# Both down-projections of a two-layer decoder wholly in pairs of chunks by seven products

## The chip, the cores and the metric

The kernel runs on one core of a Trainium2 chip. The core has TensorE (PE, the matrix engine, with its weight load shown apart as PEld), VectorE (DVE), ScalarE (ACT), GpSimd (POOL) and SyncE (SP, which only issues transfers). All of them read and write the on-chip memory; matmuls add up in eight banks of PSUM. The metric is the device time of one execution in microseconds (us).

## The reference

It is a decoder trunk of two layers over 512 tokens of width 1024. Layer 0 has a dilated attention of three head groups, layer 1 a forgetting attention (FoX) whose keys and values are projected once from the stream behind layer 0. Behind each attention stands a gated FFN with a convolution over three tokens. In short:

```python
def conv_ffn(xn, w_up, cw, cb, w_down):
    a = xn @ w_up                                   # 512 x 5632
    ap = jnp.pad(a, ((0, 0), (CONV_W - 1, 0), (0, 0)))
    a = sum(ap[:, j:j + T] * cw[j] for j in range(CONV_W)) + cb
    gate, val = jnp.split(a, 2, axis=-1)
    return (jax.nn.gelu(gate, approximate=True) * val) @ w_down   # 512 x 2816 by 2816 x 1024

for l in range(DEPTH):
    g = norm_gains[l]
    if l < N_A:
        mix = dilated_mixer(rms_norm(h, g[0]), w_qkv_a[l], w_o_a[l], cos, sin)
    else:
        if l == N_A:
            kvf = rms_norm(h, kv_norm) @ w_kvf      # keys, values, forget gates
            ...
        mix = fox_mixer(rms_norm(h, g[0]), w_q_b[j], w_o_b[j], k_sh, v_sh, c_sh)
    h = h + rms_norm(mix, g[1])
    f = conv_ffn(rms_norm(h, g[2]), w_up[l], conv_w[l], conv_b[l], w_down[l])
    h = h + rms_norm(f, g[3])
```

All is fp32. The change concerns the last product of `conv_ffn`, the down-projection, once per layer.

## The kernel before

**Products.** Every operand of a product is kept as a pair: a high part, rounded to the type that PE multiplies fast, and a low part, the rest. `mm3` (L258) makes a product of three matmuls: high by high (L259), high by low (L260), low by high (L261). A weight of 128 x 1024 is loaded raw by SP, copied to its high part by ACT (L53), and DVE subtracts that for the low part (L59). The class `Weights` (W) holds the list of all weights in the order of use and loads some of them ahead; `split` makes both parts, `take` hands out raw ones.

**Memory.** Tiles rotate through pools of fixed slots: `t8` (8 KB per partition, 17 slots), `t4` (4 KB, 9) and `t2` (2 KB, 6). Whoever asks for the next tile of a pool waits until the oldest user of that slot has finished. Each engine works off its own instructions in the order in which the program writes them.

**The down-projection.** The 2816 rows of `w_down` are 22 chunks of 128 (NF), the tokens 4 blocks of 128, the columns 2 halves of 512, so that the output fills all eight banks. ND = 8 pairs of chunks go by seven products in place of eight: a pair of chunks by two pairs of token blocks and two halves of columns is a product of 2 x 2 blocks, and sums of blocks are multiplied in the place of some blocks. The sums of the weights are made early (`down_sums`, L528: three loads, four subtractions on DVE L543 to L546, two stores) and kept in DRAM (`dT`). The sums of the activations are made in `pair_sums` (L705) from the activations that the FFN's first half stored in DRAM (`hD`, stored by POOL L610). There are two phases. In the first, `mul_one` (L752) makes four of the products of all pairs, 24 matmuls a pair. Then `combine_one` (L761) adds the banks to one another, and in the second `mul_two` (L771) adds the other three products, 18 matmuls a pair; its operands are prepared by `pair_two` (L730), from activations that stay in `t8` all the time (`dkeep`) and a fourth weight sum that `load_t4` (L725) brings back.

The 6 other chunks are plain, 24 matmuls each (`Proj`, L345): two of them between the phases, the last R = 4 at the end. For these four, `Proj.finish` (L375) runs over the blocks of tokens 0, 1, 2, 3 and their halves, 12 matmuls each, and hands each finished half to the boundary that follows. Two of the plain weights are made with an adding transfer by POOL (`high_added`, L70) in place of DVE.

**The boundary.** Behind layer 0, `SharedBoundary` (L433) takes the halves: `Mix` (L284) squares and scales them (ACT L299, DVE L306), adds the block to the stream (L313); then the block is normed (L441) and transposed (L446, low parts L463) for the values and keys. The values (`v_ps`, from L1290) start with blocks 0 and 1 while blocks 2 and 3 are still being transposed. Behind layer 1, `Final` (L474) stores the blocks; its last half is done in two parts of 256 columns.

**Where the sums of weights are made.** 16 pairs in two runs: `down0` (L1181) in the attention of layer 0, ten pairs, in `t8` tiles and stored through SP's queue, a step after each group of matmuls (L1172); `down1` (L1388) while the keys and values are made, six pairs, in `t4` tiles and stored through POOL's queue.

The few lines that set the end of the down-projection before:

```python
for b in range(NB):
    for hf in range(2):
        ...
        for i in range(self.R):
            ...
            self.step(n + i, b, hf)
        bd.half(b, hf, self.banks[b, hf])
```

Of the kernel before, what the change touches and what calls it, by code (L numbers as in the profile page):

```python
# [16 lines left out]
NB = 4  # L17
# [10 lines left out]
ND = 8  # L28
# [63 lines left out]
def trunk_kernel(ctx, tc, x, norm_gains, w_qkv_a, w_o_a, w_q_b, w_o_b, kv_norm, w_kvf, b_f,  # L92
# [62 lines left out]
    def add_ffn(l):  # L155
        for c in range(NF):
            add_cols(w_up[l], c * 128)
            add_cols(w_up[l], DFF + c * 128)

        for j in range(ND):  # L160
            add(lambda raw, j=j: [(raw[:, 0:512], w_down[l][j * 256:j * 256 + 128, 0:512]),
                                  (raw[:, 512:1024], dT[l][j, :, 0:512])])
            add(lambda raw, j=j: [(raw, dT[l][j, :, 512:1536])])
        plain = [*range(2 * ND, NF)]
        add_rows(w_down[l], [*plain[:2], *range(1, 2 * ND, 2), *plain[2:]])
# [118 lines left out]
    class Mix:  # L284
# [5 lines left out]
        def half(self, b, hf, o):  # L290
            if hf == 0:
                self.st[b] = (small(2, "ss"), t4([128, D], name="mix"), small(1, "sd"), small(1, "vr"))
            self.part(b, hf, o, H2[hf], hf == 1)
# [51 lines left out]
    class Proj:  # L345
# [3 lines left out]
        def __init__(self, KC, R, get_act, begin=0, banks=None):  # L349

            self.KC, self.R, self.get_act, self.begin = KC, R, get_act, begin
            self.w, self.banks, self.done = {}, {} if banks is None else banks, set()

        def weight(self, kc):
            while self.begin + len(self.w) <= kc:
                self.w[self.begin + len(self.w)] = W.get()
            return self.w[kc]

        def step(self, kc, b, hf, part=slice(0, 512)):
# [3 lines left out]
            c = slice(hf * 512 + part.start, hf * 512 + part.stop)  # L363
            if kc == 0:
                self.banks[b, hf] = bank([128, 512], name="acc")
            mm3(self.banks[b, hf][:, part], ah[:, s], al[:, s], w[0][:, c], w[1][:, c],
                kc == 0, kc == self.KC - 1, part.start > 0 or self.begin > 0)
# [7 lines left out]
        def finish(self, bd, ahead, hook=None):  # L375
            n = self.KC - self.R
            if hook is None:
                for kc in range(self.begin, n):
# [10 lines left out]
            for b in range(NB):  # L389
                for hf in range(2):  # L390
                    if bd.narrow == (b, hf):
                        for q, part in enumerate((slice(0, 256), slice(256, 512))):
                            for i in range(self.R):
                                self.step(n + i, b, hf, part)
                            bd.part(b, 1 + q, self.banks[b, hf][:, part], part)
                        continue
# [4 lines left out]
                    bd.half(b, hf, self.banks[b, hf])  # L401
            W.ahead = 4

    class Boundary:


        narrow = None
# [6 lines left out]
        def half(self, b, hf, o):  # L414
            self.mix.half(b, hf, o)
            if hf == 0:
                if b >= 2:
                    self.transpose(b - 2)
                if b >= 1:
                    self.norm(b - 1)  # L420
            else:
                self.mix.add(b)
# [10 lines left out]
    class SharedBoundary(Boundary):  # L433

        def __init__(self, gain_mix, gains, name):
            super().__init__(gain_mix, None, name)
            self.gains = gains

# [5 lines left out]
        def transpose(self, b):  # L446
# [13 lines left out]
            for i, xf in enumerate(xfs):  # L460
                hi, lo = self.xT[0][i][:, :, s], self.xT[1][i][:, :, s]
                act.copy(hi, xf)
                dve.tensor_tensor(lo, xf, hi.bitcast(F32), ALU.subtract)  # L463
            for i, pt in enumerate(pts):
# [9 lines left out]
    class Final:  # L474


        narrow = (NB - 1, 1)
# [7 lines left out]
        def half(self, b, hf, o):  # L485
            self.mix.half(b, hf, o)
            if hf:
                self.out(b)
# [39 lines left out]
    def down_sums(pairs, place, queue, behind):  # L528
# [3 lines left out]
        for i in range(n + 1 + behind):  # L532
# [8 lines left out]
            if 1 <= i <= n:  # L541
                a, b = live[i - 1]
# [4 lines left out]
            i -= 1 + behind  # L547
# [20 lines left out]
    def ffn(l, bd, cp, nxt, ahead):  # L568
        hD = tc.dram_tile([NF, 128, T], F32, name="hD")
        hraw, hs, hc = {}, {}, {}  # L570

        def load_h(j):
            if j < NF // 2:
                hraw[j] = t4([128, 2, T], name="hraw")
                sp.dma_start(hraw[j], hD[2 * j:2 * j + 2].rearrange("c p t -> p c t"))

        def prep(j):
            if j < NF // 2:
                load_h(j + 1)
                hs[j] = t = t8([128, 2, 2, T], F32R, name="hs")  # L580
                src = hraw.pop(j)
                act.copy(t[:, 0], src)
                dve.tensor_tensor(t[:, 1], src, t[:, 0].bitcast(F32), ALU.subtract)

        def get_act(kc):
            if kc % 2 == 0 and kc // 2 + 1 not in hs:
                prep(kc // 2 + 1)
            return hs[kc // 2][:, 0, kc % 2], hs[kc // 2][:, 1, kc % 2]
# [104 lines left out]
        keep, one, two = {}, {}, {}  # L693
        H = slice(0, 512), slice(512, 1024)

        a11, s1_, s3_, s2_, a12, a22 = (slice(i * 256, i * 256 + 256) for i in range(6))
        sums, t4r = {}, {}

        def pair_load(j):
            if j < ND:  # L700
                keep[j] = k = t8([128, 1536], name="dkeep")
                sp.dma_start(k[:, 0:512], hD[2 * j])
                sp.dma_start(k[:, 1024:1536], hD[2 * j + 1])

        def pair_sums(j):  # L705

            pair_load(j + 1)
            k = keep[j]
            dve.tensor_tensor(k[:, s3_], k[:, a11], k[:, s1_], ALU.subtract)
            dve.tensor_tensor(k[:, s1_], k[:, s1_], k[:, a22], ALU.add)  # L710
            dve.tensor_tensor(k[:, s2_], k[:, s1_], k[:, a11], ALU.subtract)

        def pair_highs(j):

            src = [*W.take(2), keep[j][:, 0:1024]]
            one[j] = [t8([128, 2, 1024], F32R, name="w") for _ in range(3)]
            for w, r in zip(one[j], src):
                act.copy(w[:, 0], r)
            sums[j] = src

        def pair_lows(j):
            for w, r in zip(one[j], sums.pop(j)):
# [7 lines left out]
        def pair_two(j):  # L730

            r1, = W.take(1)
            load_t4(j + 1)
            k, r4 = keep.pop(j), t4r.pop(j)
            w, ac = (t8([128, 2, 1024], F32R, name="w") for _ in range(2))
            t4p = t4([128, 2, 512], F32R, name="wsum")
            act.copy(w[:, 0], r1)
            dve.tensor_tensor(k[:, s2_], k[:, a12], k[:, s2_], ALU.subtract)
            act.copy(t4p[:, 0], r4)
            act.copy(ac[:, 0, 0:768], k[:, 768:1536])  # L740
            dve.tensor_tensor(w[:, 1], r1, w[:, 0].bitcast(F32), ALU.subtract)
            dve.tensor_tensor(t4p[:, 1], r4, t4p[:, 0].bitcast(F32), ALU.subtract)
            dve.tensor_tensor(ac[:, 1, 0:768], k[:, 768:1536], ac[:, 0, 0:768].bitcast(F32), ALU.subtract)
            two[j] = ac, w, t4p
# [3 lines left out]
        def product_of(o, ac, q, w, c, bp, first):  # L748
            s = slice(q * 256 + bp * 128, q * 256 + bp * 128 + 128)
            mm3(o, ac[:, 0, s], ac[:, 1, s], w[:, 0, c], w[:, 1, c], first, False, True)  # L750

        def mul_one(j, bp):  # L752
            wa, wb, ac = one[j]
# [17 lines left out]
        def mul_two(j, bp):  # L771
            ac, w, t4p = two[j]
            product_of(db[bp, 0], ac, 1, w, H[0], bp, False)
            product_of(db[bp + 2, 0], ac, 2, t4p, H[0], bp, False)
            product_of(db[bp, 1], ac, 0, w, H[1], bp, False)
# [5 lines left out]
        def down_pairs(po):  # L781
            n = 2 * ND
# [4 lines left out]
            for j in range(1, ND - 2):  # L787
# [3 lines left out]
                if j + 3 < ND:  # L791
# [3 lines left out]
                    if j + 3 == ND - 1:  # L795
                        load_h(ND)
                elif j + 3 == ND:
                    pair_lows(j + 2)
                if j == ND - 3:
                    W.high_added()  # L800
            W.high_added()
            prep(ND)
            load_t4(0)
            for bp in range(2):
                for j in (ND - 2, ND - 1):
                    mul_one(j, bp)
                combine_one(bp)
            one.clear()
            W.n_get += n
            pair_two(0)  # L810
            for bp in range(2):
                for kc in (n, n + 1):
                    for b in (bp, bp + 2):
                        po.both(kc, b)
            pair_two(1)
            for j in range(ND):
                if j < ND - 2:
                    pair_two(j + 2)
                if j == ND - 1:
                    W.n_get += ND  # L820
                if j >= ND - 2:
                    W.split(W.n_split + 2)
                for bp in range(2):
                    mul_two(j, bp)
                del two[j]
# [85 lines left out]
        po = Proj(NF, 4, get_act, 2 * ND, db)  # L911
        down_pairs(po)
        W.ahead = 4
        po.finish(nxt, ahead)
# [167 lines left out]
    def v_proj0(between):  # L1082
        banks = []
        ws = [[t.rearrange("p (k c) -> p k c", k=4) for t in W.get()] for _ in range(2)]
        for b in range(4):
# [9 lines left out]
            if b % 2:  # L1095
                act.copy(V[0][:, b - 1:b + 1, :], banks[b // 2])
                for f in between[b // 2]:
                    f()

# [47 lines left out]
    transpose0(3)  # L1147
    qk0(2, 2, 3)
    W.split(5)
    qk_post(0, 2, qk_banks[2])  # L1150
    qk0(3, 0, 1, 2, 3)
# [5 lines left out]
    def wide_proj(g, name, post, between):  # L1157

        banks = [bank([128, T], name=name) for _ in range(4)]
        for s in range(4):  # L1160
# [11 lines left out]
            next(down0, None)  # L1172
# [8 lines left out]
    down0 = down_sums([(0, j) for j in range(ND)] + [(1, j) for j in range(10 - ND)], in_one, sp, 1)  # L1181
    v_proj0([[L(qk_transpose, 0, 0), L(qk_transpose, 0, 1)],
# [97 lines left out]
    def keep_values(hf, b, o):  # L1280
        if b == 0:
# [3 lines left out]
    bd2.norm(3)  # L1285
    banks = [bank([128, 512], name="v_ps") for _ in range(4)]
    wv = []
    W.ahead = 1
    for sp_, blocks in ((0, (0, 1)), (2, (0, 1)), (0, (2,)), (2, (2,)), (0, (3,)), (2, (3,))):
# [325 lines left out]
```

## Time and profile before

| what | value |
|---|---|
| median of 3 runs | 1135.58 us (1135.26 to 1135.85) |
| the profiled execution's own time | 1135.51 us |
| its span | 1133.4 us |
| PE busy | 1120.9 us, 99% |
| DVE busy | 859.9 us, 76% |
| ACT busy | 601.4 us, 53% |
| POOL busy | 176.9 us, 16% |
| down-projection of layer 0 in the trace | 418.1 to 529.3 us |
| down-projection of layer 1 in the trace | 1017 to 1127.7 us |

The span goes from the first to the last instruction; the execution's own time is 2.1 us longer. "L259" is line 259 of the kernel above. A row of the timeline gives the start, the length, the engine, the line, the operation and the tiles (written <- read), and in brackets the idle time of the engine before it with what ended it. A row of a group gives the number of instructions, then the busy time in us and the mean of one in ns, then the idle time before them. A row of transfers gives how many there are, the size of each, and the median time from issue to landing. "dkeep", "w", "acc" and so on are the program's names of tiles.

### The profile page before, as it was taken

Reading aid. Unit: us, or ns where it says so; the run is one execution under the profiler, and the core shown is the slowest. Engines: PE = TensorE matmul, PEld = TensorE weight load, DVE = VectorE, ACT = ScalarE, POOL = GpSimd, SP = SyncE. Lnnn points to the kernel's source line nnn. Section 1 sums busy time; section 2 is a strip of 40 time slices with the busy share of each in tenths; the row PEclk is TensorE's granted clock in tenths of the full one; section 3 lists DMA queues with packets and bytes.
Section 4 is the critical chain, followed back from the end, with each engine's and each line's share of the span. In section 5 each row is a group of like instructions: output and inputs, shape, how many; then the busy total and the mean of one; then the engine's idle time right before and its main releaser. Section 6 shows DMA issues by size and latency. Waiting matters only on the chain.

```text
span 1133.4 us, 16992 instructions
## 1 busy us (share of the span) xinstructions
PE 1120.9 (99%) x6306; PEld 956.8 (84%) x6306; DVE 859.9 (76%) x1385; ACT 601.4 (53%) x1018; POOL 176.9 (16%) x259
## 2 busy tenths in 40 slices
PE   9999999999999999999999999999999999999997
PEld 6888889889899888888778888789889899888886
DVE  6558788887888588866587788848888888679754
ACT  5454565454544555655552677756444344455642
POOL 1833002200000100000001566500300000110000
PEclk9999999999999999999999999999999999999999
DMA  9269664334434778763348644363433443788732
GB/s 301 88 225 392 244 171 130 94 103 123 147 103 131 226 220 315 204 195 92 116 149 286 198 121 122 95 208 105 119 102 93 139 141 99 201 260 302 196 122 75
DMA packets 164780, 191.36 MB, mean 169 GB/s; under 512 B 9305, under 2 KB 123465, under 8 KB 164698
## 3 DMA queue, kind: packets, MB, share of 16 engines
q1 hardware_dynamic: 156442, 161.96, 45.0%
q0 software_dynamic: 8256, 28.32, 8.7%
q8 instruction: 50, 0.82, 0.3%
q14 instruction: 32, 0.26, 0.1%
HBM read 149.30 MB, written 30.46 MB: 159 GB/s over the span
## 4 chain that ended last, share of the span: by engine, by line
PE 83%; DVE 6%; issue 6%; ACT 3%; DMA 1%; POOL 1%; DVEq 0%; POOLq 0%; ACTq 0%
PE up L259 13%; PE up L260 12%; PE up L261 12%; PE acc L259 8%; PE acc L261 8%; PE acc L260 8%; PE qk_ps L260 2%; PE qk_ps L259 2%; PE qk_ps L261 2%; DVE w L59 1%; PE first L261 1%; PE first L259 1%; PE first L260 1%; PE v_ps L259 1%; PE v_ps L261 1%
## 5 line engine op out<-in xcount | busy, mean ns | idle before, releaser
L59 DVE TENSOR_TENSOR w<-wraw,w 128x1024 fp32r<-128x1024 f32 x110 | 141.1, 1301 | 34.6 <-ACT w L53 34.0
L594 ACT ACTIVATE bb<-up,conv 128x512 f32<-128x512 f32 x80 | 60.7, 776 | 153.2 <-PE up L261 77.0
L53 ACT CAST w<-wraw 128x1024 fp32r<-128x1024 f32 x110 | 112.5, 1048 | 23.8 <-DMA wraw<-in_w_up_dram 7.1
L259 PE MATMUL up<-xch,w 128*128 128x512 f32 (+1 forms) x292 | 104.9, 359 | 0.0
L260 PE MATMUL up<-xbl,w 128*128 128x512 f32 (+1 forms) x292 | 104.8, 359 | 0.0
L259 PE MATMUL up<-xbh,w 128*128 128x512 f32 (+1 forms) x292 | 104.8, 359 | 0.0
L260 PE MATMUL up<-xcl,w 128*128 128x512 f32 (+1 forms) x292 | 104.8, 359 | 0.0
L261 PE MATMUL up<-xbh,w 128*128 128x512 f32 (+1 forms) x292 | 104.7, 358 | 0.0
L261 PE MATMUL up<-xch,w 128*128 128x512 f32 (+1 forms) x292 | 104.7, 358 | 0.0
L610 POOL DMA_DIRECT2D hD<-hc x42 | 24.3, 594 | 343.4 <-DVE hc L612 343.4
L595 DVE SCALAR_TENSOR_TENSOR bb<-up,conv,bb 128x511 f32<-128x511 f32 x80 | 59.5, 743 | 20.9 <-ACT bb L594 20.9
L259 PE MATMUL acc<-w 128*128 128x512 f32 x192 | 74.7, 389 | 0.0
L260 PE MATMUL acc<-w 128*128 128x512 f32 x192 | 74.7, 389 | 0.0
L261 PE MATMUL acc<-w 128*128 128x512 f32 x192 | 74.7, 389 | 0.0
L259 PE MATMUL up<-xsh,w 128*128 128x256 f32 x224 | 63.4, 283 | 0.0
L260 PE MATMUL up<-xsl,w 128*128 128x256 f32 x224 | 63.4, 283 | 0.0
L261 PE MATMUL up<-xsh,w 128*128 128x256 f32 x224 | 63.4, 283 | 0.0
L259 PEld LDWEIGHTS up<-xch,w 128*128 128x128 f32 x292 | 55.1, 189 | 8.3
L261 PEld LDWEIGHTS up<-xbh,w 128*128 128x128 f32 x292 | 55.1, 189 | 8.3
L597 DVE SCALAR_TENSOR_TENSOR bb<-up,conv,bb 128x510 f32<-128x510 f32 x80 | 59.9, 749 | 2.8
L260 PEld LDWEIGHTS up<-xbl,w 128*128 128x128 f32 x292 | 55.1, 189 | 8.1
L259 PEld LDWEIGHTS up<-xbh,w 128*128 128x128 f32 x292 | 55.1, 189 | 8.2
(315 smaller groups left out, 3092.8 us busy)
## 6 DMA issues: line engine op xcount, KB each, us to landing
wraw<-in_w_up_dram SPq DMA_DIRECT2D x88, 512.0 KB, 4.6
wraw<-in_w_down_dram SPq DMA_DIRECT2D x28, 512.0 KB, 3.7
hD<-hc POOLq DMA_DIRECT2D x44, 256.0 KB, 4.7
dT<-dsums SPq DMA_DIRECT2D x20, 512.0 KB, 6.6
dsums<-in_w_down_dram SPq DMA_DIRECT2D x16, 512.0 KB, 7.7
dsums<-in_w_down_dram SPq DMA_DIRECT2D x32, 256.0 KB, 7.8
dkeep<-hD SPq DMA_DIRECT2D x32, 256.0 KB, 5.8
wraw<-dT SPq DMA_DIRECT2D x16, 512.0 KB, 5.9
```

The lines of the kernel that those rows point to most:

```text
L53: self.nc.scalar.copy(pair[:, 0], raw)
L59: self.nc.vector.tensor_tensor(pair[:, 1], raw, pair[:, 0].bitcast(F32), ALU.subtract)
L259: pe.matmul(o, ah, bh, start=first, stop=False, skip_group_check=shared)
L260: pe.matmul(o, ah, bl, start=False, stop=False, skip_group_check=shared)
L261: pe.matmul(o, al, bh, start=False, stop=last, skip_group_check=shared)
L594: act.activation(bb[:, s, :], ps, AF.Identity, bias=cp[:, 3, ch:ch + 1], scale=cp[:, 2, ch:ch + 1])
L595: dve.scalar_tensor_tensor(bb[:, s, 1:], ps[:, :T - 1], cp[:, 1, ch:ch + 1], bb[:, s, 1:], ALU.mult, ALU.add)
L597: dve.scalar_tensor_tensor(bb[:, s, 2:], ps[:, :T - 2], cp[:, 0, ch:ch + 1], bb[:, s, 2:], ALU.mult, ALU.add)
L610: pool.dma_start(hD[c - 1], hc.pop(c - 1))
```

## The change

All eleven pairs of chunks go by seven products (ND = 11), the plain chunks and their code are gone. Four things come with it.

First, the activations are no longer kept between the phases. The sum S2 of a pair is stored to DRAM (`sD`, through POOL's queue), and the second phase loads it again, with one chunk of activations and the fourth weight sum (`load_two`), one pair ahead. The pools have 16, 10 and 8 slots in place of 17, 9 and 6.

Second, the second phase is split into its three products, `p_21`, `p_11` and `p_12` (`p_1` is the last two). The blocks of tokens end in the order 2, 3, 0, 1. For the blocks 2 and 3, one half is already complete when the first phase's banks are added, the other ends with `p_21` of the last two pairs; `p_1` of the pairs 6 and 7 fills in behind each. For the blocks 0 and 1 the last three pairs (LAST) are held back, 9 matmuls for each half.

Third, the boundary and the values behind layer 0 follow that order, and the first four weights of the next stage are split inside the loop over the blocks, one for each.

Fourth, 22 weight sums are made. Two pairs are loaded right behind the first transposes of layer 0's attention, in `t4` tiles (`sums`); `down0` has ten pairs, with two steps between load and subtraction; `down1` seven pairs, from the values on; `down2`, new, has the last three pairs of layer 1 at the end of FoX attention.

```diff
-ND = 8
+ND = NF // 2
+LAST = 3
...
-    p8 = ctx.enter_context(tc.tile_pool(name="p8", bufs=17))
-    p4 = ctx.enter_context(tc.tile_pool(name="p4", bufs=9))
-    p2 = ctx.enter_context(tc.tile_pool(name="p2", bufs=6))
+    p8 = ctx.enter_context(tc.tile_pool(name="p8", bufs=16))
+    p4 = ctx.enter_context(tc.tile_pool(name="p4", bufs=10))
+    p2 = ctx.enter_context(tc.tile_pool(name="p2", bufs=8))
...
         def pair_sums(j):
...
             dve.tensor_tensor(k[:, s2_], k[:, s1_], k[:, a11], ALU.subtract)
+            pool.dma_start(sD[j], k[:, s2_])
...
-        def load_t4(j):
+        def load_two(j):
             if j < ND:
-                t4r[j] = t2([128, 512], name="dt4")
-                sp.dma_start(t4r[j], dT[l][j, :, 1536:2048])
+                later2[j] = k, r4 = t4([128, 768], name="dact2"), t2([128, 512], name="dt4")
+                sp.dma_start(k[:, 0:256], sD[j])
+                sp.dma_start(k[:, 256:768], hD[2 * j + 1])
+                sp.dma_start(r4, dT[l][j, :, 1536:2048])
...
+            last = range(ND - LAST, ND)
+            for j in range(2, ND - 2):
+                for bp in range(2):
+                    p_21(j, bp)
+                if 2 <= j - 2 < ND - LAST - 2:
+                    p_1(j - 2, 0)
+                    p_1(j - 2, 1)
+                    two.pop(j - 2)
+                pair_two(j + 3)
+            W.n_get += 3 * ND
+            for i, b in enumerate(nxt.order):
+                if ahead and i < 3:
+                    W.split(W.n_split + 1)
+                if b >= 2:
+                    nxt.half(i, 0, 1, db[b, 1])
+                    for j in range(ND - 2, ND):
+                        p_21(j, b - 2)
+                    nxt.half(i, 1, 0, db[b, 0])
+                    for bp in range(2):
+                        p_1(last[0] - 2 + i, bp)
+                    continue
+                for j in last:
+                    p_11(j, b)
+                nxt.half(i, 0, 0, db[b, 0])
+                if ahead and i == 3:
+                    W.split(W.n_split + 1)
+                parts = (slice(0, 256), slice(256, 512)) if nxt.narrow and i == NB - 1 else (slice(0, 512),)
+                for q, part in enumerate(parts):
+                    for j in last:
+                        p_12(j, b, part)
...
     class SharedBoundary(Boundary):
...
+        order = (2, 3, 0, 1)
...
+            if (i, n) == (3, 0):
+                self.transpose(self.order[1], lambda: self.norm(self.order[2]))
+            elif n == 0 and i >= 1:
+                self.norm(self.order[i - 1])
...
+            if (i, n) == (2, 1):
+                self.transpose(self.order[0])
...
-    def down_sums(pairs, place, queue, behind):
+    def down_sums(pairs, place, queue, lag, behind):
...
+    sums = down_sums([(0, 0), (0, 1)], in_two, sp, 1, 0)
...
-    down0 = down_sums([(0, j) for j in range(ND)] + [(1, j) for j in range(10 - ND)], in_one, sp, 1)
+    down0 = down_sums([(0, j) for j in range(2, ND)] + [(1, 0)], in_one, sp, 2, 1)
...
+    down1 = down_sums([(1, j) for j in range(1, 8)], in_two, pool, 1, 0)
...
-    down1 = down_sums([(1, j) for j in range(10 - ND, ND)], in_two, pool, 0)
...
+    down2 = down_sums([(1, j) for j in range(8, ND)], in_two, pool, 1, 0)
...
+        if n in (N - 1, N, N + 1, N + 2):
+            next(down2)
```

More of the change, by code (lines that the diff above doesn't have):

```diff
@@ L463, in transpose @@
                 dve.tensor_tensor(lo, xf, hi.bitcast(F32), ALU.subtract)
+            if later is not None:
+                later()
             for i, pt in enumerate(pts):
@@ L1150, in trunk_kernel @@
     qk_post(0, 2, qk_banks[2])
+    next(sums)
     qk0(3, 0, 1, 2, 3)
@@ L1171, in wide_proj @@
                 f()
-            next(down0, None)
+            if (g, name, s) != (1, "qk_ps", 1):
+                next(down0, None)
     def v_post(g, b, o):
```

234 lines of the change are left out of this document (108 added, 126 removed).

## The prediction

> **What bounds the kernel now.** I read the page's totals first, then the chain that ended last, then what TensorE waits for, then windows over the stages that the change touches, and single rows last.
>
> ```profile
> span 1133.4 us, 16992 instructions
> PE 1120.9 (99%) x6306; PEld 956.8 (84%) x6306; DVE 859.9 (76%) x1385; ACT 601.4 (53%) x1018; POOL 176.9 (16%) x259
> PE 83%; DVE 6%; issue 6%; ACT 3%; DMA 1%; POOL 1%; DVEq 0%; POOLq 0%; ACTq 0%
> ```
>
> TensorE (PE) is busy 99% of the span and is 83% of the chain. Its waits, by what it waited for (total us, times, longest), are these, longest first:
>
> ```profile
> PE o_ps L1503 <- ACT pT L1490: 1.5, 1, 1.5
> PE warm L220 <- DVE zero L215: 1.4, 1, 1.4
> PE acc L259 <- DVE mix L306: 1.1, 1, 1.1
> PE qk_ps L260 <- DVE w L59: 1.0, 2, 0.8
> ```
>
> None of them is in a down-projection except the third, at the kernel's end. So the time is the count of matmuls times their pitch: a matmul taken out is worth its pitch, unless something that was hidden comes late. The question is only what comes late. The windows give the length of the stretch, then busy time and count of PE, weight loads, DVE, ACT and POOL, then clock, share of the DMA engines, GB/s. The first two are the down-projection of layer 0: its first products, and all after them up to the next stage.
>
> ```profile
> 418.10:461.60 43.50, 43.50 (x193) 36.04 (x192) 33.87 (x44) 25.50 (x28) 2.30 (x3) 1.00 0.81 265
> 461.60:529.30 67.70, 67.28 (x305) 55.65 (x304) 52.01 (x72) 41.29 (x64) 0.00 (x0) 1.00 0.51 153
> ...
> 70.00:130.00 60.00, 59.84 (x336) 49.82 (x335) 45.84 (x114) 27.81 (x82) 18.09 (x32) 1.00 0.95 352
> 100.00:105.00 5.00, 5.00 (x28) 3.94 (x28) 3.46 (x4) 2.76 (x5) 3.69 (x7) 1.00 1.03 415
> ```
>
> The first says 192 matmuls in 43.5 us, 0.2266 us each, at clock 1.00. DVE, the third pair of numbers, is busy 33.87 of them (78%) and 52.01 of 67.7 (77%): it is the engine to watch. The last two are the attention of layer 0, where the DMA engines are nearly full.
>
> **The saving.** A pair of chunks costs 4 x 2 x 3 = 24 matmuls of first products and 3 x 2 x 3 = 18 of second ones, 42 in all, where two plain chunks cost 48. Three pairs per layer change over: 18 matmuls fewer per layer. In layer 1 the last half block runs in two parts of 256 columns; it shrinks from 4 chunks to 3 pairs' product, 2 x 3 matmuls of 256 columns fewer (as 3 wide ones), so 15 wide and 6 narrow.
>
> ```profile
> 1123.61 0.28 PE L261 MATMUL acc<-w,hs 128*128 128x256 f32 x1
> ...
> 1124.69 0.28 PE L261 MATMUL acc<-w,hs 128*128 128x256 f32 x1
> ```
>
> These stand nine matmuls apart: 1.08 / 9 = 0.12 us. Layer 0: 18 x 0.2266 = 4.08; layer 1: 15 x 0.2266 + 6 x 0.12 = 4.12. Together -8.2 us.
>
> The Trainium skill, page TensorE: Matmul & The Clock Gate, section Back-to-back issue gap, gives a sustained 131 ns for a matmul of 512 columns between weight loads. By it the 36 would save an estimated 4.7 us; the trace disagrees, at 227 ns.
>
> **First products, then second ones: are weights and activations ready?** DVE per pair:
>
> ```profile
> 425.82 0.42 DVE L709 TENSOR_TENSOR dkeep<-dkeep 128x256 f32<-128x256 f32 x1
> ...
> 439.79 0.42 DVE L709 TENSOR_TENSOR dkeep<-dkeep 128x256 f32<-128x256 f32 x1
> ...
> 462.71 0.70 DVE L769 TENSOR_TENSOR acc<-acc,dsum 128x512 f32<-128x512 f32 x1
> 467.40 0.42 DVE L738 TENSOR_TENSOR dkeep<-dkeep 128x256 f32<-128x256 f32 x1
> ...
> 479.18 0.41 DVE L738 TENSOR_TENSOR dkeep<-dkeep 128x256 f32<-128x256 f32 x1
> ```
>
> L709 opens a pair of the first phase; three pairs lie between the rows: 13.97 / 3 = 4.66 us, against 24 x 0.2266 = 5.44 us of PE. Three more pairs at 4.66 stay under PE's pace: nothing. L738 opens a pair of the second phase; four pairs: 11.78 / 4 = 2.95 us of DVE against 18 x 0.2266 = 4.08 of PE. The first phase ends at 418.1 + 264 x 0.2266 = 477.9. The last sum (L769) ended at 463.41, 1.8 us behind its phase; so after the change at about 479.9. From there eight pairs of the second phase remain for DVE (3 to 10): 479.9 + 8 x 2.95 = 503.5. PE asks for pair 10 after 36 (pairs 0, 1) + 42 (p_21 of 2 to 8) + 48 (p_1 of 2 to 5) + 3 (p_21 of pair 9) = 129 matmuls: 477.9 + 29.2 = 507.1. Slack 3.6 us; a pitch of 3.4 us a pair uses it up. On this side the plain chunks' cover is gone (they gave PE work while the second products' operands were made), and it is replaced by eight pairs' p_21 and p_1 running behind each other.
>
> What can make the pitch longer is the loading: per pair now the weight row (512 KB), a chunk of activations (256), the sum S2 from DRAM (128) and the weight sum (256), 1.18 MB. At the 415 GB/s of the window 100 to 105 that is 2.84 us, at the 352 of 70 to 130 3.35, at the 265 of the first phase 4.45, though there the engines were busy only 0.81 (327 at full share, 3.61). I take 3.35, the nearest row with full engines: just inside. For the first pairs, whose loads start while phase one still loads, +0.3 us; bounds 0 and the rival below.
>
> The Trainium skill, page DMA: Bandwidth & Descriptors, section Bandwidth, puts transfers of 1 MB at 341 GB/s and advises to batch to 1 MiB or more, while these are 128 to 512 KB. By its figure a pair takes an estimated 3.46 us, some 0.4 us a layer late; the window of 415 GB/s, in transfers no larger, says that the size alone does not hold it there.
>
> **Stores by POOL.** 22 stores of S2 at some 0.58 us each are 12.8 us on an engine that is busy 16%; in layer 0's first phase it had 2.30 us of work in 43.5. Hidden, 0. The reload of S2 on SP waits for its store; behind it on SP stand that pair's two other loads and the next weights, but the store of pair 0 is nearly a whole first phase old by then, and of pair 10 several pairs' time.
>
> ```profile
> L610 POOL DMA_DIRECT2D hD<-hc x42 | 24.3, 594 | 343.4 <-DVE hc L612 343.4
> ```
>
> **The end of down 0.** Here lies the one cost that I expect on the path. Four weights of the next stage are split inside the loop over blocks, where before that was done ahead of it:
>
> ```profile
> 500.45 2.50 DVE L59 TENSOR_TENSOR w<-wraw,w 128x1024 fp32r<-128x1024 f32 x2 [1.98 <-ACT w L53]
> ...
> 510.77 0.60 ACT L299 ACTIVATE junk<-acc 128x512 bf16<-128x512 f32 x1 [2.03 <-PE acc L261]
> ...
> 539.51 1.29 DVE L463 TENSOR_TENSOR xkl<-xf,xkh 128x512 fp32r<-128x512 f32 x2
> ...
> 541.11 0.39 PE L259 MATMUL v_ps<-w,xkh 128*128 128x512 f32 x1
> ```
>
> and the same stretch as a window:
>
> ```profile
> 505.00:541.00 36.00, 35.58 (x170) 29.46 (x169) 23.27 (x43) 19.73 (x45) 0.00 (x0) 1.00 0.34 86
> ```
>
> From the read of the first block's second half (510.77) to the first low part of the third transposed block (539.51 + 0.65) the chain of mix, norm and transposes takes 29.4 us; PE has matmuls to cover it until 541.1, 30.3 us. After the change each of the last two blocks' halves is 9 instead of 12 matmuls, the cover shorter by some 6 x 0.2266 = 1.4: 28.9. Alone, the unchanged chain of 29.4 makes PE wait 0.5. Now the splits: 4 x 1.25 = 5.0 us of DVE (and 4 x 1.05 of ACT). In the window 505 to 541 DVE is idle 12.7 us, so all could hide (0.5 in all), or none (5.5), since that idle time sits inside the chain's own steps. The first two go ahead of blocks whose matmuls still leave a block's time, the others directly into the steps of the third and fourth: I take two of four, 0.5 + 2.5 = +3.0 us. The changed order of blocks (2, 3, 0, 1) only renames which transposes are last. In layer 1 nothing is split there, and the tail behind the last matmul stays: 0.
>
> **Weight sums at other places.** A pair's sums are four DVE instructions of 692 to 716 ns (first and last row):
>
> ```profile
> L543 DVE TENSOR_TENSOR dsums<-dsums 128x512 f32<-128x512 f32 x16 | 11.5, 716 | 0.0
> ...
> L546 DVE TENSOR_TENSOR dsums<-dsums 128x512 f32<-128x512 f32 x16 | 11.4, 711 | 0.9 <-DMA dsums<-in_w_down_dram 0.4
> ```
>
> Where the added ones go (a window, then single rows), and what a store of sums takes to land:
>
> ```profile
> 27.00:48.00 21.00, 21.00 (x146) 19.59 (x145) 9.75 (x9) 7.58 (x10) 20.84 (x22) 1.00 0.01 2
> ...
> 559.73 1.39 DVE L1265 TENSOR_TENSOR kst<-k_ps,kst 64x512 fp32r<-64x512 f32 x2 [6.67 <-ACT kst L1262]
> ...
> 746.03 0.69 DVE L1517 TENSOR_TENSOR OTb<-o_ps,OTb 128x512 fp32r<-128x512 f32 x1 [7.56 <-ACT OTb L1513]
> ...
> 762.36 0.60 ACT L299 ACTIVATE junk<-acc 128x512 bf16<-128x512 f32 x1 [1.71 <-PE acc L261]
> ...
> dT<-dsums SPq DMA_DIRECT2D x20, 512.0 KB, 6.6
> ```
>
> Six more pairs at some 2.8 us. Two are loaded in 27 to 48, where the DMA engines are 0.01 busy and DVE 46%; of ten in layer 0's attention (as many as before) only the place changes, in 16 slots instead of 17. One falls behind the values stage, whose keys leave DVE idle 6.67 us at a time. Three fall at the end of FoX attention: 8.5 us against one idle gap of 7.56, with w_o's weights queued on SP behind slots that a store holds 6.6 us (on POOL's queue, where these stores stand, nothing else is due until the next FFN's sums); ahead of 762.36 ACT idles 1.71 us for PE there, so a weight may come that much later. I take +0.3 for attention (-0.5 to +3, a store's half landing) and +0.4 for FoX (0 to +3).
>
> **Sum.** The profiled run took 1135.51 us (span 1133.4 and 2.1 around it), 0.07 below the median. 1135.5 - 8.2 + 0.3 (second products) + 3.0 (end of down 0) + 0.3 + 0.4 = 1131.3. About 0.2%, 2.3 us, is what a measurement of this kernel can tell from no change.
>
> **Rivals.** *The second products' loads bind.* Place: behind the last combine, both layers. At 4.45 us a pair (265 GB/s) pair 10 is ready at 479.9 + 35.6 = 515.5, 8.4 us late: two layers +16.8, 1148. It ends on the slower side from 3.41 + (4.2 + 2.3) / 16 = 3.8 us a pair, 310 GB/s. For it: the first phase moved 265; against it: 352 held for 60 us, and SP loads as far ahead as ten slots allow.
>
> *A slot late in attention 0 or at the end of FoX.* A weight's copy waits for a slot that a store of sums holds: one landing of 6.6 us less some 2 us of lead, 4.6: 1135.9, no change. In both places: 1140, slower. For it: 0.95 of the DMA engines' time taken there, one slot fewer; against it: PE waits there now only 1.0 us on a weight.
>
> *The boundary is fully exposed.* None of the splits hides, and the other two terms stand at their half: 1131.3 + 2.5 + 1.5 = 1135.3, no change.
>
> *A matmul taken out is worth less than its pitch*, since what runs beside it sets the pace: if each of the 33 wide and 6 narrow ones is worth only the 0.12 us of the narrow rows, they save 4.7, not 8.2: 1134.8, no change. The row of 192 matmuls in 43.5 us speaks against it. The figure that the Trainium skill's page TensorE: Matmul & The Clock Gate gives in the section Back-to-back issue gap comes to the same.
>
> **Chances.** Forecast 0.66. Loads bind 0.12 (slower). A slot late once 0.10 (same), twice 0.04 (slower). Boundary exposed 0.05 (same). Pitch 0.03 (same). Faster 0.66, same 0.18, slower 0.16. The forecast's own range: 1131.3 - 2.5 (splits hidden) - 1.5 (the others at their low ends) = 1127.3, up to 1134.5. The range to 1136.2 takes in the cases of no change and leaves the slower ones, 0.16, out.
>
> **What would show it.** Right: 528 matmuls of first products for the two layers at 0.227, the second phase without PE gaps, a gap of some 3 us at the third block of the values stage waiting for xkl, PE's sum of busy time 8 us less. Wrong: PE waiting in the second phase on the low parts (DVE) or on loads; gaps on w in the attention of layer 0 or at w_o; the splits found wholly in DVE's idle time (then 1128.3).

## The result, and the profile after

The changed kernel takes 1139.56 us (1139.24 to 1142.58), the one before 1135.58: a ratio of 1.0041, interval 1.0026 to 1.0056. It is slower by 4 us, where 1131.3 was forecast.

The totals of the page of the changed kernel, then its longest waits of TensorE:

```profile
span 1137.3 us, 17235 instructions
PE 1118.0 (98%) x6267; PEld 951.0 (84%) x6267; DVE 909.4 (80%) x1455; ACT 611.2 (54%) x1032; POOL 191.8 (17%) x285
```

```profile
PE o_ps L1535 <- ACT pT L1522: 2.6, 5, 1.5
PE v_ps L260 <- DVE w L60: 2.3, 2, 2.0
...
PE s_ps L1013 <- DVE qkT L989: 1.1, 1, 1.1
...
PE xt_ps L327 <- DVE xn L278: 1.0, 1, 1.0
PE pT_ps L1520 <- DVE nm L1496: 0.8, 2, 0.4
PE acc L260 <- DVE w L60: 0.8, 1, 0.8
PE v_ps L259 <- ACT xkh L470: 0.7, 1, 0.7
```

PE has 39 matmuls fewer, and waits that were not there before: for a weight's low part in the values of layer 0's attention (`v_ps` L260), for `qkT`, `xn`, `w` in w_o (`acc` L260), more often for `pT`. A stage is taken from its first matmul to the next stage's first one (attention 0: from the span's start; FoX: first scores to last output; w_o 1: from there to the FFN's first matmul; the tail: to the span's end). All stages of the two profiled executions, in us:

| stage | before | after | difference |
|---|---|---|---|
| attention 0 | 145.56 | 150.85 | +5.3 |
| w_o 0 and FFN 0 up | 272.52 | 272.54 | 0.0 |
| down 0 | 111.24 | 106.52 | -4.7 |
| values behind layer 0 | 23.56 | 25.87 | +2.3 |
| keys and second values | 81.12 | 81.10 | 0.0 |
| FoX loop | 111.09 | 113.10 | +2.0 |
| w_o 1 | 35.12 | 38.09 | +3.0 |
| FFN 1 up | 237.08 | 237.06 | 0.0 |
| down 1 and tail | 116.14 | 112.19 | -4.0 |

The down-projections gave what they should, 8.7 us. The four other differences add up to 12.6. The two phases of down 0 in the changed kernel, as windows, show that the new second phase has no hole: PE is busy through both, at clock 1.00.

```profile
423.40:483.22 59.82, 59.82 (x265) 49.54 (x264) 54.90 (x73) 36.83 (x41) 5.39 (x10) 1.00 0.83 292
483.22:529.90 46.68, 46.68 (x215) 38.82 (x214) 41.22 (x61) 32.88 (x54) 0.00 (x0) 1.00 0.69 228
```

The loss in the values behind layer 0 shows as two waits, for a low part of a weight and for a transposed block, and the rest, 1.3 us, as matmuls that stand further apart:

```profile
537.86 0.50 PE L260 MATMUL v_ps<-w,xkh 128*128 128x512 f32 x1 [0.29 <-DVE w L60]
543.59 0.50 PE L259 MATMUL v_ps<-w,xkh 128*128 128x512 f32 x1 [0.67 <-ACT xkh L470]
```

The largest loss is at the start of attention 0. DVE, POOL, SP and ACT of the changed kernel there:

```profile
31.42 1.61 DVE L554 TENSOR_TENSOR dsums<-dsums 128x512 f32<-128x512 f32 x1
33.06 1.46 DVE L555 TENSOR_TENSOR dsums<-dsums 128x512 f32<-128x512 f32 x1
34.56 1.46 DVE L556 TENSOR_TENSOR dsums<-dsums 128x512 f32<-128x512 f32 x1
36.05 1.51 DVE L557 TENSOR_TENSOR dsums<-dsums 128x512 f32<-128x512 f32 x1
37.48 2.11 DVE L60 TENSOR_TENSOR w<-wearly,w 128x1024 fp32r<-128x1024 f32 x1
...
63.76 0.69 DVE L554 TENSOR_TENSOR dsums<-dsums 128x512 f32<-128x512 f32 x1
```

```profile
28.25 1.13 POOL L960 CAST xpl<-xal 128x512 fp32r<-128x512 f32 x1
...
32.41 1.56 POOL L960 CAST xph<-xah 128x512 fp32r<-128x512 f32 x1
33.92 1.55 POOL L960 CAST xpl<-xal 128x512 fp32r<-128x512 f32 x1
35.41 1.60 POOL L960 CAST xph<-xah 128x512 fp32r<-128x512 f32 x1
```

```profile
34.55 3.36 SPq L562 DMA_DIRECT2D dT<-dsums  x2
38.01 1.25 SPq L46 DMA_DIRECT2D wraw<-in_w_qkv_a_dram  x2
```

```profile
44.06 1.05 ACT L54 CAST w<-wraw 128x1024 fp32r<-128x1024 f32 x1 [6.42 <-DMA wraw<-in_w_qkv_a_dram]
```

A subtraction of weight sums takes 0.69 us at 63.76, when POOL is idle, and 1.46 to 1.61 at 31 to 37 us, when POOL reorders the activations. POOL's casts take 1.55 to 1.60 there instead of 1.13, and their starts fall between DVE's starts: the two engines go one after the other. So the four subtractions take 6.1 us, not 2.8, and the low part of the weight behind them starts at 37.48. In the kernel before it started at 32.34, as DVE's row there says:

```profile
32.34 1.28 DVE L59 TENSOR_TENSOR w<-wearly,w 128x1024 fp32r<-128x1024 f32 x1 [0.77 <-ACT w L53]
```

PE waits. SP stands at the store of these sums, the loads of the next weights go out behind it, and ACT idles 6.42 us for them. And the wait costs more than its length:

```profile
39.65 0.38 PE L260 MATMUL v_ps<-w,xah 128*128 128x256 f32 x1 [2.03 <-DVE w L60]
```

```profile
38.00:39.00 1.00, 0.00 (x0) 0.00 (x0) 1.00 (x1) 0.00 (x0) 1.00 (x2) 1.00 0.64 250
...
40.00:41.00 1.00, 1.00 (x10) 1.00 (x9) 0.98 (x1) 0.00 (x0) 1.00 (x1) 0.80 0.95 250
41.00:42.00 1.00, 1.00 (x6) 1.00 (x6) 0.00 (x0) 0.00 (x0) 0.92 (x4) 0.50 0.68 153
42.00:43.00 1.00, 1.00 (x7) 1.00 (x6) 0.00 (x0) 0.00 (x0) 0.95 (x3) 0.50 0.82 221
43.00:44.00 1.00, 1.00 (x7) 1.00 (x7) 0.00 (x0) 0.00 (x0) 0.97 (x2) 0.50 1.02 364
44.00:45.00 1.00, 1.00 (x10) 1.00 (x10) 0.00 (x0) 0.94 (x1) 1.00 (x2) 1.00 0.98 379
```

After it the granted clock is 0.50 for some 3.4 us (0.80 and three times 0.50), 1.7 us more. Of the 5.3 us of this stage 3.7 are this wait and this clock; a later wait of 1.1 us at 95.9 for `qkT` makes most of the rest.

The Trainium skill, page SBUF — State Buffer, section SBUF: two separate sides, says that a DVE instruction with two inputs in SBUF and a GpSimd instruction that reads SBUF take a shared pair of ports in turn, each for its whole length. The alternating starts above agree.

### The profile page after: what moved, and what is told of

Read it like the earlier page. It is cut to its first block, busy times and chain, and to the rows that moved or that the text cites. A ratio compares the mean times of both kernels' runs of the same rounds, so it can differ in the third digit from the quotient of the medians.

```text
span 1137.3 us, 17235 instructions
## 1 busy us (share of the span) xinstructions
PE 1118.0 (98%) x6267; PEld 951.0 (84%) x6267; DVE 909.4 (80%) x1455; ACT 611.2 (54%) x1032; POOL 191.8 (17%) x285
## 5 line engine op out<-in xcount | busy, mean ns | idle before, releaser
L60 DVE TENSOR_TENSOR w<-wraw,w 128x1024 fp32r<-128x1024 f32 x102 | 131.7, 1312 | 42.5 <-ACT w L54 42.1
L54 ACT CAST w<-wraw 128x1024 fp32r<-128x1024 f32 x102 | 104.2, 1048 | 45.5 <-DMA wraw<-in_w_qkv_a_dram 19.4
L259 PE MATMUL acc<-w 128*128 128x512 f32 (+1 forms) x311 | 120.6, 388 | 1.1 <-DVE mix L306 1.1
L261 PE MATMUL acc<-w 128*128 128x512 f32 (+1 forms) x311 | 120.4, 387 | 0.0
L260 PE MATMUL up<-xbl,w 128*128 128x512 f32 (+1 forms) x292 | 104.8, 359 | 0.0
L260 PE MATMUL up<-xcl,w 128*128 128x512 f32 (+1 forms) x292 | 104.8, 359 | 0.0
L260 PE MATMUL acc<-w 128*128 128x512 f32 (+1 forms) x267 | 103.2, 387 | 0.0
L259 PEld LDWEIGHTS acc<-w 128*128 128x128 f32 x311 | 58.4, 188 | 13.1 <-DVE mix L306 1.3
L261 PEld LDWEIGHTS acc<-w 128*128 128x128 f32 x311 | 58.4, 188 | 11.9
L260 PE MATMUL up<-xsl,w 128*128 128x256 f32 x224 | 63.4, 283 | 0.0
L259 PEld LDWEIGHTS up<-xbh,w 128*128 128x128 f32 x292 | 55.1, 189 | 8.3
```

Of the source, the lines that this page charges most:

```text
L54: self.nc.scalar.copy(pair[:, 0], raw)
L60: self.nc.vector.tensor_tensor(pair[:, 1], raw, pair[:, 0].bitcast(F32), ALU.subtract)
L259: pe.matmul(o, ah, bh, start=first, stop=False, skip_group_check=shared)
L260: pe.matmul(o, ah, bl, start=False, stop=False, skip_group_check=shared)
L261: pe.matmul(o, al, bh, start=False, stop=last, skip_group_check=shared)
```

## The experiments

The columns of the stages (in us) are those of the table above, from each run's profiled execution, one for each run. "Time" is the median of the executions, beside 1135.6 to 1135.7 for the kernel before in the same jobs. Times of one kernel spread by up to 7 us, and the slower ones have the lower mean clock (a5_both: 1134.26 us at 0.998, 1141.06 at 0.994), so the stages carry the readings. A stage in which the clock was halved for 3.4 us is 1.7 us longer by that alone. In the executions shown this came once in attention 0 (after, a2, a4, a5, f1), twice (a1) and three times (v1), once in the FoX loop (a1, a5, v1, c1) and once in w_o 1 (a1, p1).

| run | attention 0 | values | FoX loop | w_o 1 | time | ratio to before, interval |
|---|---|---|---|---|---|---|
| before | 145.56 | 23.56 | 111.09 | 35.12 | 1135.58 | |
| after | 150.85 | 25.87 | 113.10 | 38.09 | 1139.56 | 1.0041 (1.0026 to 1.0056) |
| a1_split_first | 152.87 | 25.91 | 115.00 | 40.49 | 1143.82 | 1.0072 (1.0057 to 1.0087) |
| a2_sums_late | 152.03 | 25.88 | 113.62 | 38.65 | 1142.54 | 1.0061 (1.0046 to 1.0076) |
| a3_twelve_in_down0 | 146.81 | 25.87 | 113.75 | 38.76 | 1136.28 | 1.0008 (0.9999 to 1.0017) |
| a4_store_later | 149.14 | 25.87 | 114.22 | 39.01 | 1139.63 | 1.0031 (1.0018 to 1.0044) |
| a5_both | 148.93 | 25.90 | 114.77 | 38.88 | 1136.96 | 1.0013 (1.0000 to 1.0026) |
| f1_t8 | 150.27 | 25.87 | 113.36 | 35.80 | 1137.84 | 1.0022 (1.0011 to 1.0033) |
| p1_p4_9 | 151.59 | 25.91 | 111.02 | 39.66 | 1139.84 | 1.0034 (1.0022 to 1.0046) |
| v1_splits_ahead | 155.02 | 24.39 | 113.35 | 38.64 | 1140.25 | 1.0038 (1.0024 to 1.0053) |
| b1_before_slots | 145.69 | 23.56 | 113.22 | 35.12 | 1138.76 | 1.0028 (1.0018 to 1.0039) |
| c1_all | 146.92 | 24.43 | 112.42 | 35.47 | 1130.35 | 0.9953 (0.9936 to 0.9969) |

**The start of attention 0: order on DVE.**

```diff
-    next(sums)
     qk0(3, 0, 1, 2, 3)
     W.ahead = 4
     W.split(6)
+    next(sums)
```

> The changed kernel with one edit: in the attention of layer 0 the sixth weight is split ahead of the first four subtractions of weight sums, not behind them. Theory A (order on DVE): the changed kernel's PE gap of 2.1 us at 37.3 us and the 3.3 us at half clock behind it come from that weight's low part, which stood behind subtractions of 1.5 us each; both go, first matmul of w_o comes 3.5 us or more earlier (150.9 to about 147), time about 1136. Rival B (loads): the weights of that stage are late because SP stands at the stores of the sums and the DMA engines are full; then the gap only moves a few us later and the time stays within 1 us of 1139.6.

Attention 0 took 152.87 us, 2 more than with the change alone. The gap at 37 us went, as theory A had it, and a larger one of 5.4 us came at 49.0 us, as rival B had it. ACT of this run:

```profile
36.25 2.00 ACT L54 CAST w<-wraw 128x1024 fp32r<-128x1024 f32 x2
48.52 1.04 ACT L54 CAST w<-wraw 128x1024 fp32r<-128x1024 f32 x1 [10.27 <-DMA wraw<-in_w_qkv_a_dram]
```

Its wait for the next weight grew to 10.27 us: SP stands at the store of sums until 39.6 us and then issues the loads of more sums ahead of the weights. The low part of that weight stands on DVE ahead of the copy of `qkT` for which PE waits. Behind the larger gap the clock was 0.50 from 52.8 to 59.6 us, 3.4 us more. Theory A was half of it.

**The same, later.**

```diff
-    next(sums)
     qk0(3, 0, 1, 2, 3)
...
-             [L(qk_transpose, 0, 2), L(qk_transpose, 0, 3), L(scores, 0, 0), L(scores, 0, 1)]])
+             [L(qk_transpose, 0, 2), L(qk_transpose, 0, 3), L(scores, 0, 0), L(scores, 0, 1), L(next, sums)]])
```

> The changed kernel with one edit: the second and third step of the two early pairs of sums (subtract, store, load the second pair) come later, behind the first and second pair of blocks of the first value product, when POOL's reordering is over for the most part. Theory A, as it stands after the runs so far (SP's queue is what binds: the stores of sums wait there for subtractions that take 1.5 us each beside POOL, and the loads of the next weights stand behind them): no store waits on SP at 35 to 38 us, ACT gets the next weights before 40 us, the PE gap of 2.1 us at 37 us and the half clock behind it go, the attention of layer 0 takes 146 to 148 us, not 150.9. Rival B (two more pairs are more bytes than the stage can load before its weights): the gap only moves to a later place, attention 150 us or more.

152.03 us: nothing is late at 37 us, but PE waits 2.6 us at 92.6 for `qkT`, with a clock of 0.66 over 95 to 100 behind it, and 1.2 at 125.1. The time is what rival B said; its cause, the bytes, is not shown by it. With its 4 KB slots held to 55 us and later, the run does not tell bytes from slots.

**The store's place in SP's queue, alone and with the order.**

```diff
-    sums = down_sums([(0, 0), (0, 1)], in_two, sp, 1, 0)
+    sums = down_sums([(0, 0), (0, 1)], in_two, sp, 1, 1)
...
-             [L(qk_transpose, 0, 2), L(qk_transpose, 0, 3), L(scores, 0, 0), L(scores, 0, 1)]])
+             [L(qk_transpose, 0, 2), L(qk_transpose, 0, 3), L(scores, 0, 0), L(scores, 0, 1), L(next, sums)]])
```

This is a4_store_later; a5_both has the edit of a1_split_first besides.

> The changed kernel with one edit: the stores of the two early pairs of sums stand one step later in SP's queue, behind the loads of the weights that follow. The subtractions stay where they are. Theory A2 (two waits in a row at the start of attention: DVE's order makes the gap at 37 us, and SP's queue, standing at the store, makes the weights behind it late): the gap of 2.1 us at 37 us stays, since its weight was loaded long before, but ACT's wait of 6.4 us for the next weight shrinks to 3 us or less; attention 149 to 150 us. Rival B (bytes or slots make the weights late, not the order of the queue): ACT's wait stays at 6 us, attention 150.5 or more.

> The changed kernel with two edits: the sixth weight is split ahead of the early subtractions (which alone only moved the gap, 5.4 us at 48.7 us, attention 152.9), and the stores of these sums stand one step later in SP's queue. Theory A2: with both waits gone there is no gap over 1 us ahead of 60 us, attention 147 to 148. Rival B (slots: the four 4 KB tiles of the sums are held still longer, so the weights find none): the gap at 48 us stays 3 us or more, attention 151 or more.

ACT in a4_store_later, and in a5_both:

```profile
39.63 2.00 ACT L54 CAST w<-wraw 128x1024 fp32r<-128x1024 f32 x2 [1.96 <-DVE w L60]
```

```profile
39.38 1.05 ACT L54 CAST w<-wraw 128x1024 fp32r<-128x1024 f32 x1 [0.88 <-DMA wraw<-in_w_qkv_a_dram]
```

With the store behind the weights' loads, ACT's wait of 6.4 us for a load is gone: the queue's order made it, not the bytes. The gap at 37 us stays in a4 (2.00 us) and goes in a5, where the weight is ahead of the subtractions too. So there are two waits in a row here, PE's at 37 us and ACT's behind it, and each was seen to go with its own edit; with ACT's the wait of 1.1 us at 95.9 went too. But a5 is at 148.93, not 147 to 148: a wait of 1.7 us for `qkT` at 91.9 with a clock of 0.50 from 94.2 to 97.6 behind it is left, and what makes this copy late was not tested.

**The early pairs given up.**

```diff
-    sums = down_sums([(0, 0), (0, 1)], in_two, sp, 1, 0)
-    next(sums)
...
-    down0 = down_sums([(0, j) for j in range(2, ND)] + [(1, 0)], in_one, sp, 2, 1)
-    next(down0)
+    down0 = down_sums([(0, j) for j in range(ND)] + [(1, 0)], in_one, sp, 1, 1)
...
```

Load and subtraction are one step apart here, where the change had two for `down0`.

> The changed kernel with one edit: no early pairs; all twelve pairs of the attention of layer 0 go one after the other through 8 KB slots, loads and subtractions one step apart, as the kernel before did with ten. Theory A (the early pairs' place is what costs): the gap at 37 us goes, attention takes 146 to 148 us. Rival B (the bytes): 2.4 us more of loading and storing in 70 to 130 us, where the DMA engines are full, show as gaps there, 149 us or more. Rival C (the slots): with 16 slots of 8 KB a weight waits for a store, ACT's waits on slots grow.

146.81 us: theory A. The same twelve pairs, 16 slots and bytes cost 1.25 us over before in the saturated stage (one wait of 1.2 us at 119.9), and 5.3 with two of them at the start. Their place, with the one step less between load and subtraction, made 4.0 us, and 3.3 us of the time.

**The end of FoX.** ACT of the changed kernel at w_o 1, and below it with this edit:

```diff
-    down2 = down_sums([(1, j) for j in range(8, ND)], in_two, pool, 1, 0)
+    down2 = down_sums([(1, j) for j in range(8, ND)], in_one, pool, 1, 0)
```

> The changed kernel with one edit: the three pairs of weight sums at the end of FoX attention take 8 KB slots, not 4 KB slots. Theory A (slots): w_o's weights came late there because the sums hold six of the ten 4 KB slots until their stores land; with other slots ACT's waits for w_o (2.7, 4.2, 2.0 us) go and the stretch from the last output of FoX to the first product of the FFN falls from 38.1 to 35 to 36 us: time about 1137. Rival B (DVE's 8.5 us of subtractions) or C (DMA bandwidth, the same bytes in the same place): the stretch stays at 38 us.

```profile
750.77 1.05 ACT L54 CAST w<-wraw 128x1024 fp32r<-128x1024 f32 x1
754.50 1.05 ACT L54 CAST w<-wraw 128x1024 fp32r<-128x1024 f32 x1 [2.67 <-DMA wraw<-in_w_o_b_dram]
759.78 1.05 ACT L54 CAST w<-wraw 128x1024 fp32r<-128x1024 f32 x1 [4.23 <-DMA wraw<-in_w_o_b_dram]
762.83 1.05 ACT L54 CAST w<-wraw 128x1024 fp32r<-128x1024 f32 x1 [2.00 <-DMA wraw<-in_w_o_b_dram]
```

```profile
750.44 3.89 ACT L54 CAST w<-wraw 128x1024 fp32r<-128x1024 f32 x4
```

All four weights of w_o are there when ACT comes to them, and w_o 1 takes 35.80 us in place of 38.09. The twelve subtractions on DVE are the same (742.78 to 751.2) and so are the bytes: rivals B and C fall, the 4 KB slots were it for these 2.3 us; 0.7 of the 3.0 is left.

**The FoX loop.** The diff touches its code only at the end, where `down2` takes its steps; in the trace the loop is 1.9 us late by 733 us, and the first of those subtractions comes at 743.1.

```diff
-    p4 = ctx.enter_context(tc.tile_pool(name="p4", bufs=10))
+    p4 = ctx.enter_context(tc.tile_pool(name="p4", bufs=9))
```

> The changed kernel with one edit: nine 4 KB slots, not ten. Theory A: the FoX loop (first scores to last output) took 113.1 us against 111.1 before, though nothing in it was edited, because the tenth slot lets POOL make the bias earlier, so that it falls beside DVE's instructions of the softmax; with nine slots it takes 111 to 111.5 us. At the end of FoX the slots are scarcer by one: w_o later by 1 us or more. Time 1138 to 1140. Rival B: the loop is longer for another cause (transfers, other slots): it stays at 113.

And the reverse, the kernel before with the slots of the change:

> The kernel before with one edit: 16, 10 and 8 slots in place of 17, 9 and 6. Theory A: ten 4 KB slots alone make the FoX loop 2 us longer, 113.1 us in place of 111.1; the rest stays; time about 1137.5. Rival B: the slots alone change nothing, 1135.6, and the loop's 2 us come from what the change puts before it.

Nine slots: 111.02 us, the time of before. The slots of the change in the kernel before, which has no `down2`: 113.22, slower by 3 us in all (0.5 us more in each down-projection). So the tenth 4 KB slot costs 2 us there. The time of p1_p4_9 did not fall with it: in its profiled execution attention 0 and w_o 1 took 2.3 us more. The 1.6 at w_o are no sign of scarcer slots, since the clock was 0.50 from 765.4 to 768.8 us, which is 1.7.

How the slot costs it is less sure. POOL's waits before it makes the bias, in the kernel before, the changed one and p1_p4_9:

```profile
POOL bias L1438 <- DVE nm L1464: 16.6, 12, 1.9
```

```profile
POOL bias L1470 <- DVE nm L1496: 4.5, 6, 0.8
```

```profile
POOL bias L1470 <- DVE nm L1496: 15.3, 12, 1.9
```

With ten slots POOL waits less and makes the bias at other times, beside other instructions of DVE's softmax. DVE's scaling of `prob` at 128x512 takes 616 ns in the mean in the changed kernel and 615 in b1_before_slots, against 553 before and 573 in p1_p4_9; but in sum over the 64 scalings that is about 1 us more than before, and which of PE's waits it makes is open. That part of the expectation is not shown, only that the slot is the cause.

**The splits at the end of down 0.**

```diff
             W.n_get += 3 * ND
+            W.split(W.n_split + ahead)
             for i, b in enumerate(nxt.order):
-                if ahead and i < 3:
-                    W.split(W.n_split + 1)
...
-                if ahead and i == 3:
-                    W.split(W.n_split + 1)
```

> The changed kernel with one edit: the four weights of the values are split ahead of the loop over blocks at the end of down-projection 0, not one in each round. Theory A: the low parts stand in the chain of mix, norm and transposes, and the fourth comes late for the values (PE gaps of 0.45 and 0.84 us); ahead of the loop they go into time that DVE has, and the values' first part takes 23.6 to 24.5 us, not 25.9: time 1138. Rival B: the engines have no such time ahead of the loop, the first block's mix starts later by up to 5 us and the same is lost: within 0.5 us of 1139.6.

The values take 24.39 us, 1.5 less, without their two gaps, and down 0 stays at 106.52: theory A for that stage. The time did not fall. The profiled execution was the slowest of five (1142.77 us): its attention 0, which the edit does not touch, took 155.02 us, with a clock of 0.82 and 0.50 over 95 to 105 us behind a wait of 2.2 us, as well as 0.66 over 40 to 45. Why the median, 1140.25, did not fall is not shown; the stage is what can be read.

**All four together:** the edits of a3_twelve_in_down0, p1_p4_9, f1_t8 and v1_splits_ahead.

> The changed kernel with four edits together: twelve pairs in one run in the attention of layer 0, nine 4 KB slots, the last three pairs of sums in 8 KB slots, the four splits ahead of the loop over blocks. If the costs are what theory A says and stand each by itself: attention 147, values 24.4, FoX loop 111.0, w_o 35.8, and the saving in the two down-projections kept: 1139.6 - 3.5 - 1.5 - 2.1 - 2.3 = about 1130. Rival: the costs come from one lack (bytes or slots) and only move between the stages: 1135 or more.

1130.35 us, faster than both. TensorE's longest waits in it:

```profile
PE o_ps L1527 <- ACT pT L1514: 2.1, 2, 1.5
PE warm L220 <- DVE zero L215: 1.3, 1, 1.3
PE s_ps L1010 <- DVE qkT L986: 1.2, 1, 1.2
PE acc L259 <- DVE mix L306: 1.1, 1, 1.1
```

The costs stand for the most part by themselves: they did not move elsewhere when each was taken away. Attention 146.92, values 24.43 and w_o 35.47 are as expected; only the FoX loop, 112.42, is 1.3 over before. That is the clock and not the slot: behind the wait of 1.5 us in the first row, which the kernel before has too, it was halved here for 3.4 us, worth 1.7.

```profile
717.60:721.00 3.40, 3.40 (x18) 2.60 (x14) 3.37 (x7) 2.10 (x7) 1.38 (x3) 0.50 0.55 137
```

## Why the prediction was wrong

It said faster, 1131.3, with 0.66; it came out slower, 1139.56, outside the range.

**The saving** was right: 8.2 us worked out, 8.7 found, since a gap of 0.42 us at the second block's transposes (525.2 us in the kernel before) also went; 4.7 in down 0 against 4.08, 3.95 in layer 1 against 4.12. The count fell by 39 as worked out. PE's sum of busy time fell by only 2.9 us where 8 was named as a sign, because matmuls at half clock, or further apart by short waits, count as busy: 2.0 us more of it in attention 0, 1.1 to 1.3 each in the values, the FoX loop and w_o.

**Second products' loads**: right, and the rival with the loads fell. No PE gap in the second phase, with 228 GB/s and 0.69 of the DMA engines' time. The 0.4 us a layer that the Trainium skill's page DMA: Bandwidth & Descriptors, section Bandwidth, would make of it was not seen.

**Stores by POOL**: hidden, as said; no wait of PE in a down-projection names them.

**The end of down 0**: +3.0 was said, +2.3 measured. Without the splits in the loop +0.8 is left (v1), so 0.5 for the cover was near and 2.5 for two splits of four was 1.5. The one gap of 3 us for `xkl` that was named as a sign did not come; the waits were 0.29 for a weight and 0.67 for `xkh`.

**Weight sums at other places** is the step that failed, at +0.3 and +0.4 against +5.3 and +3.0. For attention the window 27 to 48 us was quoted because DMA was 0.01 busy and DVE 46%, but the same row has POOL busy 20.84 of 21 us, and the two engines delay one another. The 2.8 us were taken from means of 692 to 716 ns, of rows that are nearly all 0.69 us long. Nor did the working put the moved instructions into the queues: what stands behind the subtractions on DVE (the sixth weight), and behind the store on SP (the next weights). And behind the wait of 2.0 us the clock took 1.7 more, which no term had.

For the end of FoX the rival's mechanism was right (w_o's weights behind slots that sums hold) and its chance too low. The DVE idle gap of 7.56 us did hide the subtractions; it was the wrong resource to look at. The rival "a slot late in both places" gave 1140, near the 1139.56 measured, but by luck: its mechanism held at FoX, not in attention, where order and clock did it, and 2.0 us came from the FoX loop, which it does not have.

**The slots** were not priced at all. The change of 9 to 10 was named in the text as slots that SP may load ahead into, as if more of them could only help; it cost 2.0 us in a loop that the diff touches only at its end.

## What to carry to other kernels

Work moved into an engine's idle time needs three looks more than that idle time: what stands behind it in the same queues (its loads and stores in SP's too), whose slots it holds until its store lands, and whether POOL runs beside a DVE instruction with two inputs, which here then took twice as long (0.69 us against 1.46 to 1.61). A change of pool sizes is a part of the change and may move every stage that rotates through them; run the old kernel with the new sizes. When a gain that is certain in one stage does not come, a table by stages shows where it went.

## What was not expected of the hardware

A TensorE gap of 1.5 to 2 us may halve the clock: 0.50 for about 3.4 us behind 2.0 us in the changed kernel, in f1_t8, a4_store_later and v1_splits_ahead (0.66 to 0.68 over 40 to 45 us), and not in p1_p4_9, behind a gap as long at the same place (its row is the second, that of f1_t8 the first):

```profile
40.00:45.00 5.00, 5.00 (x31) 5.00 (x31) 1.12 (x1) 0.91 (x1) 4.84 (x10) 0.66 0.91 265
```

```profile
40.00:45.00 5.00, 5.00 (x45) 5.00 (x44) 0.96 (x1) 1.00 (x1) 4.84 (x9) 1.00 0.90 277
```

A wait of 1.5 us in the FoX loop left the clock at 1.00 in the kernel before and in the changed one, and was followed by 0.50 for 3.4 us in c1_all and v1_splits_ahead.

The Trainium skill, page TensorE: Matmul & The Clock Gate, section What's actually happening, has a clock that falls to half after an idle window of about 3.4 us, and a window that runs freely. That the same gap halves the clock in one run and not in another agrees with the free window; that 1.5 to 2 us are enough does not agree with a whole idle window.
